# Stores one step behind, and two products ahead of their copies, in the first layer of a streaming-encoder trunk

## The chip, the cores and the metric

The kernel runs on one core of a Trainium2 chip. The metric is the device time of one execution in microseconds. An execution of the kernel before is described by its median over three runs and by one execution that the hardware profiler recorded; the rows below are of that one.

## What is computed

The reference is a trunk of two layers over 2048 frames of 1024 channels, in float32. The change lies in the first layer, a gated mixer, and in the lines that prepare the second:

```
h = rms_norm(x, a_norm_g)
u, v, z = split(h @ w_in, 3)                    # 3 x 2048 channels
u = gelu(u);  v = layer_norm(gelu(v), ln_g, ln_b)
mixed = einsum('hts,bgshc->bgthc', w_m, v)      # 16 heads, groups of 128 frames
y = u * (mixed + b_s) * silu(z)
x = x + y @ w_out
```

`w_m` is a 128x128 matrix per head, zero where a frame would see a later chunk of 64. The second layer is attention over bands of nine chunks, and a final norm follows; it is not changed.

## The kernel before

**Products.** Each float32 operand is split into a high and a low float32r part (`split`, L264: ScalarE copies the high part, VectorE subtracts for the low one), and each product is three matmuls (`mm3`, L105 to L108: high x high, high x low, low x high). The large products of the first layer use seven sub-products in place of eight (a Strassen scheme): `PH = (1, 2, 6, 5, 7, 4, 3)` names the phases, and each phase has its own combination T of weight quarters and its own combination S of input blocks.

**Steps.** The first layer is one list of steps (weight block n, phase, row pair j), written out by hand and run by `run_steps` (L461). One step is one accumulator, or two in the phases 1 and 2 of block 0, which serve the blocks 0 and 1 together: 12 matmuls of 128x512 each (24 in the output product). Three steps ahead (`LOOK`) the S of a step is prepared: transposed and split from the normed x (`s_split`, L409) in block 0, or loaded (`s_load`, L402) later on. Each split S is also stored to HBM (`hsd`, L416), since the blocks 1 to 5 read it again. Blocks 0 and 1 give v, which is stored after the gelu (`done_v`, L435; store at L440). Blocks 2 to 5 give u and z for 512 channels each; they need v mixed over the frames.

**Mixing.** `mix` (L614) makes one bank: an accumulator tile of 128 x 2 x 2 x 128, which holds the products of two heads, three matmuls of 128x256 each. In its loop the three matmuls of a head are followed by the copy of that half to SBUF by ScalarE (L628, scale and bias included), and then come the next head's. There are two such tiles in turn. A bank's result `m` is multiplied into u (`merge_u`, L632, on GpSimd) or into the gate (`done_uz`). `transposes` (L636) turns the finished y and stores it (L643). The output product reads y back and stores the new residual x1 (`done_out`, L842; store at L851).

**Late work.** `later(k, f)` (L425) keeps f for k steps; `flush(s)` (L428) runs what is due at the start of the products of step s. Evictions follow their product at once; gelus are a step late, stores of v two steps late with their statistics.

**Order.** Nearly all loads and stores are issued by SyncE's queue (SP), in program order. The listed order isn't the final one: a scheduler places the instructions of each engine by data and by listing, so that what is listed later may still stand earlier. An instruction that waits for its data holds those behind it on its engine. Buffers are rings: six S tiles (L242), four raw weight tiles, eight T tiles, four transpose tiles, four accumulators for products.

**Preparing the second layer.** `load_scaled` (L169) loads a weight block, multiplies it by a norm gain on GpSimd and stores the scaled block for later use (L178). Five such calls are listed within the output product of the first layer; later calls come from the second layer.

Of the kernel before, what the change touches and what calls it, by code (L numbers as in the profile page):

```python
# [17 lines left out]
P = 128  # L18
# [5 lines left out]
TB = T // P  # L24
# [9 lines left out]
def trunk_kernel(  # L34
# [19 lines left out]
    nc = tc.nc  # L54
# [4 lines left out]
    x1d = [dram.tile([T, D], F32, name=f"x1d{t}") for t in range(NT)]  # L59
# [45 lines left out]
    def mm3(ps, lh, ll, rh, rl, first, last):  # L105
        mm(ps, lh, rh, start=first, stop=False)  # L106
        mm(ps, lh, rl, start=False, stop=False)  # L107
        mm(ps, ll, rh, start=False, stop=last)  # L108
# [19 lines left out]
    def norm_transpose(name, src, wide, pool, tag, bufs):  # L128
# [37 lines left out]
            norm(b)  # L166
        return [(th[:, k, :], tl[:, k, :]) for k in range(KD)], block

    def load_scaled(src, name, gain=None, keep=None):  # L169
        raw = sh.tile([P, 1024], F32, tag="raw", name=f"raw_{name}", bufs=4)  # L170
        nc.sync.dma_start(raw[:], src)
        if gain is not None:
            k = gain.shape[1]
            r3 = raw[:].rearrange("p (k c) -> p k c", k=k)
            nc.gpsimd.tensor_tensor(
                r3, r3, gain.broadcast_to([P, k, 1024 // k]), op=ALU.mult
            )
            nc.sync.dma_start(keep, raw[:])  # L178
        return raw

    def load_split(*args):
# [37 lines left out]
    with ExitStack() as actx:  # L219
# [8 lines left out]
        vd = {  # L228
            (c, r, q): dram.tile([P, 2, 512], F32, name=f"vd{c}_{r}_{q}")
            for c in range(4) for r in range(2) for q in range(4)  # L230
        }
        ytd = {
            (r, c, j): dram.tile([P, 2, 512], F32, name=f"ytd{r}_{c}_{j}")
            for r in range(2) for c in range(2) for j in range(NJ)
        }
# [3 lines left out]
        def acc_tile(name):  # L239
            return ca.tile([P, 512], F32, tag="acc", name=name, bufs=25)  # L240

        def s_tile(name):  # L242
            return ca.tile([P, 2, 4, P], F32R, tag="S", name=name, bufs=6)
# [20 lines left out]
        def split(hi, lo, src, key=None):  # L264
            ins = nc.scalar.copy(hi, src)
            if key:
                in_order(key, ins)
            nc.vector.tensor_tensor(lo, src, hi.bitcast(F32), op=sub)  # L268
# [130 lines left out]
        def s_views(t):  # L399
            return [(t[:, 0, k, :], t[:, 1, k, :]) for k in range(4)]  # L400
# [8 lines left out]
        def s_split(ph, j, rows):  # L409

            pt = ptp[0].tile([P, 4, P], F32, tag="t0", name=f"t0_{ph}_{j}", bufs=4)
            for k in range(4):
                tpose(pt[:, k, :], rows[:, k * P : k * P + P], ident[:])
            t = s_tile(f"S0_{ph}_{j}")
            split(t[:, 0], t[:, 1], pt[:], "S")
            nc.sync.dma_start(  # L416
                hsd[ph, j][:], t[:].rearrange("p a k c -> p a (k c)").bitcast(F32)
            )
            return s_views(t)


        late = []
        now = [0]

        def later(steps, f_):  # L425
            late.append((now[0] + steps, f_))

        def flush(s):  # L428
            now[0] = s
            due = [f_ for at, f_ in late if at <= s]  # L430
            late[:] = [x_ for x_ in late if x_[0] > s]
            for f_ in due:
                f_()

        def done_v(n, r, c, j, t):  # L435
            ch = 2 * n + c

            def close():
                nc.vector.bn_stats(vst[:, r, j, ch, :], t)
                nc.sync.dma_start(vd[ch, r, j // 2][:, j % 2, :], t)  # L440

            later(1, lambda: nc.scalar.activation(t, t, AF.Gelu_apprx_tanh))
            later(2, close)
# [17 lines left out]
        def run_steps(steps, ts, prep, act, events):  # L461


            left = {}
            for s in range(-LOOK, len(steps)):
                for f_ in events.get(s, []):
                    f_()
                if s >= 0:
                    act(s, *steps[s], left.pop(s))
                if s + LOOK < len(steps):  # L470
                    left[s + LOOK] = prep(*steps[s + LOOK])
                for f_ in ts.get(s, []):
                    f_()
# [62 lines left out]
        def block_d(j):  # L536
            s_split(5, j, hb.pop(j)[:, 0:512])
# [76 lines left out]
        def mix(n, r, q, part):  # L614
            vh, vl = mixp[n, r, q]
            ws = wsp[n]
            if part == 0:
                mt[n, r, q] = up[0].tile([P, 2, 512], F32, tag="m", name=f"m{n}_{r}_{q}", bufs=4)
            m = mt[n, r, q]
            px = up[1].tile([P, 2, 2, P], F32, tag="mx", name=f"mx{n}_{r}_{q}_{part}", bufs=2)  # L620
            for i in range(2):
                h = 2 * part + i
                c = slice(h * P, h * P + P)
                mm3(
                    px[:, i], ws[:, 0, h, :], ws[:, 1, h, :], vh[:, :, c], vl[:, :, c], True, True
                )
                hh = (n - 2) * 4 + h
                nc.scalar.activation(  # L628
                    m[:, :, c], px[:, i], AF.Identity, scale=0.5, bias=bsh[:, hh : hh + 1]
                )  # L630
# [5 lines left out]
        def transposes(n, r, j, y):  # L636
            pt = up[1].tile([P, 4, P], F32, tag="ty", name=f"ty{n}_{r}_{j}", bufs=2)
            for h in range(4):
                tpose(pt[:, h, :], y[:, h * P : h * P + P], ident[:])
            yo = up[2].tile([P, 512], F32, tag="yo", name=f"yo{n}_{r}_{j}", bufs=2)  # L640
            nc.scalar.copy(yo[:], pt[:].rearrange("p a b -> p (a b)"))
            fc = n - 2
            nc.sync.dma_start(ytd[r, fc // 2, j][:, fc % 2, :], yo[:])  # L643

        def done_uz(n, r, c, j, t):
            tt = nc.vector.tensor_tensor
            if c == 0:
                later(1, lambda: nc.scalar.activation(t, t, AF.Gelu_apprx_tanh))
                if r == 0:
                    u0[n, j] = t  # L650
                    return
                later(2, lambda: tt(t, t, z1[n][:, j, :], op=mul))
            else:
                th = up[2].tile([P, 512], F32, tag="th", name=f"th{n}_{r}_{j}", bufs=2)
                m = mt[n, 1, j // 2][:, j % 2, :] if r else u0[n, j]
                eng = nc.gpsimd if r else nc.vector
                later(1, lambda: nc.scalar.activation(th[:], t, AF.Tanh, scale=0.5))
                later(2, lambda: nc.vector.scalar_tensor_tensor(t, th[:], 1.0, t, op0=add, op1=mul))
                later(2, lambda: eng.tensor_tensor(t, t, m, op=mul))
                if r == 1:  # L660
                    return
            later(4, lambda: transposes(n, r, j, t))
# [92 lines left out]
        for n in range(2, 6):  # L755
# [3 lines left out]
            for r, offs in ((0, (5, 9, 13, 17)), (1, (22, 25, 28, 31))):  # L759
                for q, o in enumerate(offs):  # L760
# [4 lines left out]
                    if r == 0:  # L765
                        for i in range(2):
                            j = 2 * q + i
# [5 lines left out]
        def act_in(s, n, ph, j, views):  # L773
            flush(s)
            for m in (0, 1) if n == 0 and ph in (1, 2) else (n,):
                ps = pmm.tile([P, 512], F32, tag="mm", name=f"P{m}_{ph}_{j}")
                product(ps, views, tops[m, ph])
                if m < 2:
                    evict(m, ph, j, ps, done_v, None if m else c22_0)
                else:  # L780
                    evict(m, ph, j, ps, done_uz, uz_c22(m))
# [60 lines left out]
        def done_out(n, r, c, j, t):  # L842
            blk = 2 * j + r
            cs = slice(c * 512, c * 512 + 512)
            xr = acc_tile(f"xr{blk}_{c}")
            nc.sync.dma_start(xr[:], x[blk * P : (blk + 1) * P, cs])
            rs = slice(blk % TB * P, (blk % TB + 1) * P)

            def close():
                (tg if r and c else tv)(t, t, xr[:], op=add)  # L850
                nc.sync.dma_start(x1d[blk // TB][rs, cs], t)  # L851

            later(1, close)

# [26 lines left out]
        for c in range(3):  # L881
            at(nin + 26 + 2 * c, lambda c=c: load_scaled(*kqz_source(0, 0, c)))
        for c in range(2):
            at(nin + 32 + 2 * c, lambda c=c: load_scaled(*v_source(0, 0, c)))
# [8 lines left out]
        def prep(n, ph, j):  # L893
            return prep_out(ph, j) if n == "o" else prep_in(n, ph, j)

        def act(s, n, ph, j, views):
            if n == "o":
                act_out(s, ph, j, views)
            else:
                act_in(s, n, ph, j, views)  # L900

        run_steps(steps, ts, prep, act, events)
        flush(1 << 30)
        blocks[0](3)
        px.close()

# [487 lines left out]
```

## Time and profile before

| | us |
|---|---|
| median of three runs | 2729.15 |
| lowest and highest | 2726.96, 2733.49 |
| the profiled execution, whole | 2726.1 |
| its span, first to last instruction | 2724.1 |

The first layer's blocks take about the first half of the span, up to about 1390 us. Around the span lie 2.0 us. A row of the page's groups gives a source line, an engine, the operation with the tiles it writes and reads, and then the busy time; a row of a timeline gives the start and the length in microseconds, the engine, the line and the operation, and in brackets how long the engine had been idle before it and what ended that. PE stands for TensorE's matmuls, PEld for its weight loads, DVE for VectorE, ACT for ScalarE, POOL for GpSimd, SPq for SyncE's queue.

### The profile page before, as it was taken

What the parts mean: (1) busy time and instruction counts of PE and PEld (TensorE: products, weight loads), DVE (VectorE), ACT (ScalarE), POOL (GpSimd) and SP (SyncE); (2) the same over time, 40 slices, a digit from 0 to 9 for tenths busy, and PEclk for the clock granted to TensorE, in tenths of its full rate; (3) what the DMA queues carried; (4) which work ended last, traced back from release to release, by engine and by line L of the source; (5) the groups of instructions that cost most, each with busy time, mean ns of one, the idle gap of its engine ahead of it and who ended that gap; (6) DMA issues with size and microseconds to landing.
All of it is one profiled execution on the core that took longest, in us unless ns stands there. A gap on an engine that the chain in (4) does not pass through costs nothing.

```text
span 2724.1 us, 39971 instructions
## 1 busy us (share of the span) xinstructions
PE 2666.4 (98%) x14176; PEld 2268.7 (83%) x14176; DVE 1932.2 (71%) x3211; ACT 1274.6 (47%) x2244; POOL 711.9 (26%) x767
## 2 busy tenths in 40 slices
PE   8999999999999999999999999999999999999997
PEld 6788878878788888777888888899988999889996
DVE  5655666766667667666767666877778777787777
ACT  5422243433433434232245554566655666556663
POOL 3512123141231422632034430211202112021111
PEclk9999999999999999999999999999999999999999
DMA  8899988886877868758767655544454444453332
GB/s 291 307 335 332 324 324 314 286 299 234 309 263 249 312 232 323 270 200 290 258 220 233 217 181 178 166 146 153 154 174 164 148 151 154 150 160 119 115 112 70
DMA packets 209190, 607.16 MB, mean 223 GB/s; under 512 B 24288, under 2 KB 24288, under 8 KB 208992
## 3 DMA queue, kind: packets, MB, share of 16 engines
q1 hardware_dynamic: 208992, 604.62, 64.5%
q8 instruction: 113, 1.85, 0.3%
q14 instruction: 85, 0.70, 0.1%
HBM read 466.11 MB, written 127.93 MB: 218 GB/s over the span
## 4 chain that ended last, share of the span: by engine, by line
PE 42%; DVE 5%; DMA 4%; POOL 1%; issue 1%; ACT 1%; SPq 0%; DVEq 0%; POOLq 0%; ACTq 0%
PE pj L106 6%; PE pj L107 6%; PE pj L108 6%; PE s L1065 4%; PE tp L1104 4%; PE pv L1131 4%; PE bo L108 2%; PE bo L107 2%; PE bo L106 2%; PE vp L108 2%; PE vp L106 2%; PE vp L107 2%; DMA xr<-in_x 1%; DMA bx_b<-x1d 1%; DMA A<-ytd 1%
## 5 line engine op out<-in xcount | busy, mean ns | idle before, releaser
L106 PE MATMUL P<-T,S 128*128 128x512 f32 x1248 | 497.4, 399 | 6.5 <-ACT x L376 4.5
L108 PE MATMUL P<-T,S 128*128 128x512 f32 x1248 | 490.6, 393 | 0.0
L107 PE MATMUL P<-T,S 128*128 128x512 f32 x1248 | 489.5, 392 | 1.1 <-DVE T L268 1.1
L1084 POOL TENSOR_SCALAR pr<-pr,sl 128x640 f32<-128x640 f32 (+4 forms) x256 | 199.1, 778 | 754.6 <-DVE sl L1083 662.0
L1080 ACT ACTIVATE pr<-pr,nm 128x640 f32<-128x640 f32 (+4 forms) x256 | 195.5, 764 | 270.6 <-DVE nm L1073 269.0
L106 PE MATMUL pj<-hh_b,wh_b 128*128 128x512 f32 x768 | 311.5, 406 | 0.7 <-ACT hh_b L160 0.7
L107 PE MATMUL pj<-hl_b,wh_b 128*128 128x512 f32 x768 | 302.2, 394 | 0.0
L108 PE MATMUL pj<-hh_b,wl_b 128*128 128x512 f32 x768 | 301.3, 392 | 0.0
L108 PEld LDWEIGHTS P<-T,S 128*128 128x128 f32 x1248 | 235.5, 189 | 50.5
L106 PEld LDWEIGHTS P<-T,S 128*128 128x128 f32 x1248 | 236.1, 189 | 49.2 <-ACT x L376 4.7
L107 PEld LDWEIGHTS P<-T,S 128*128 128x128 f32 x1248 | 236.3, 189 | 43.9 <-DVE T L268 1.3
L1108 DVE TENSOR_TENSOR pt<-tp,pt 128x640 fp32r<-128x640 f32 (+4 forms) x256 | 188.8, 737 | 60.0 <-ACT pt L1107 57.4
L1073 DVE CUSTOM_DVE_ANT_0 pr<-s,bias 128x640 f32<-128x640 f32 (+4 forms) x256 | 188.3, 735 | 45.9 <-PE s L1065 42.2
L108 PEld LDWEIGHTS pj<-hh_b,wl_b 128*128 128x128 f32 x768 | 144.2, 188 | 33.2
L1107 ACT CAST pt<-tp 128x640 fp32r<-128x640 f32 (+4 forms) x256 | 159.1, 622 | 22.5 <-PE tp L1104 17.2
L1104 PE MATMUL tp<-ident,pr 128*128 128x128 f32 x1120 | 164.8, 273 | 3.3 <-DVE pt L1108 1.6
L106 PEld LDWEIGHTS pj<-hh_b,wh_b 128*128 128x128 f32 x768 | 144.6, 188 | 19.6 <-ACT hh_b L160 0.9
L1104 PEld LDWEIGHTS tp<-ident,pr 128*128 128x128 f32 x1120 | 134.6, 140 | 31.3 <-issue 3.1
L107 PEld LDWEIGHTS pj<-hl_b,wh_b 128*128 128x128 f32 x768 | 145.0, 189 | 17.4
L106 PE MATMUL vp<-wh_bv,hh_b 128*128 128x256 f32 x512 | 148.0, 289 | 0.8 <-ACT hh_b L160 0.8
L108 PE MATMUL vp<-wh_bv,hl_b 128*128 128x256 f32 x512 | 145.4, 284 | 0.1
L107 PE MATMUL vp<-wl_bv,hh_b 128*128 128x256 f32 x512 | 144.8, 283 | 0.0
(216 smaller groups left out, 6063.3 us busy)
## 6 DMA issues: line engine op xcount, KB each, us to landing
S<-hsd SPq DMA_DIRECT2D x288, 512.0 KB, 4.9
rw<-in_w_a SPq DMA_DIRECT2D x108, 512.0 KB, 5.8
raw_b<-wk SPq DMA_DIRECT2D x75, 512.0 KB, 4.0
A<-ytd SPq DMA_DIRECT2D x72, 512.0 KB, 5.1
hsd<-S SPq DMA_DIRECT2D x56, 512.0 KB, 4.5
rwo<-in_w_out SPq DMA_DIRECT2D x40, 512.0 KB, 5.3
bias<-reld SPq DMA_DIRECT2D x64, 320.0 KB, 3.2
raw_bo<-in_wb_out SPq DMA_DIRECT2D x36, 512.0 KB, 3.9
```

Of the source, the lines that this page charges most:

```text
L106: mm(ps, lh, rh, start=first, stop=False)
L107: mm(ps, lh, rl, start=False, stop=False)
L108: mm(ps, ll, rh, start=False, stop=last)
L1065: mm(ps[:, sg, :w], q[:, qb * P : (qb + 1) * P], kx[:, koff + sg * w : koff + (sg + 1) * w], start=i == 0, stop=i == 1,)
L1073: nc.vector.tensor_tensor_reduce(out=pr[:, c0:].rearrange("p (a b) -> p a b", a=nseg), in0=ps[:, :nseg, :w], in1=bias[:, c0:].rearrange("p ...
L1080: nc.scalar.activation(pr[:, c0:], pr[:, c0:], AF.Exp, scale=-1.0, bias=nm[:], accum_out=sl[:])
L1084: nc.gpsimd.tensor_scalar(pr[:, c0:], pr[:, c0:], sl[:], 1.0, op0=ALU.mult, op1=ALU.mult)
L1104: tpose(tp[:, b, :], pr[:, b * P : (b + 1) * P], ident[:])
L1107: nc.scalar.copy(oh, tp[:, b0:5, :])
L1108: nc.vector.tensor_tensor(pt[:, 1, b0 + qq : 5 + qq, cs], tp[:, b0:5, :], oh.bitcast(F32), op=ALU.subtract)
L1131: mm(po[:, 0, :], keys(i), pt[:, j, i, :], start=(t == 0 and j == 0 and i == blocks[0]), stop=(j == 1 and i == blocks[-1]),)
```

## The change

In the first layer each store that used to be listed right behind the operation whose result it takes is now listed one step later: the S stores, the v stores, the y stores and the x1 stores. The stores of scaled weights are listed two steps later while the first layer's steps run (`put_off` holds a function then, and is emptied at their end). At the end of the steps, what is still kept is run step by step, so that work which keeps further work is run too. In `mix`, the matmuls of both heads of a bank are listed first, and then the two copies.

```
+    put_off = []
+
     def load_scaled(src, name, gain=None, keep=None):
...
-            nc.sync.dma_start(keep, raw[:])
+            if put_off:
+                put_off[0](lambda: nc.sync.dma_start(keep, raw[:]))
+            else:
+                nc.sync.dma_start(keep, raw[:])
...
             split(t[:, 0], t[:, 1], pt[:], "S")
-            nc.sync.dma_start(
+            later(1, lambda: nc.sync.dma_start(
                 hsd[ph, j][:], t[:].rearrange("p a k c -> p a (k c)").bitcast(F32)
-            )
+            ))
...
                 nc.vector.bn_stats(vst[:, r, j, ch, :], t)
-                nc.sync.dma_start(vd[ch, r, j // 2][:, j % 2, :], t)
+                later(1, lambda: nc.sync.dma_start(vd[ch, r, j // 2][:, j % 2, :], t))
...
-            for i in range(2):
-                h = 2 * part + i
-                c = slice(h * P, h * P + P)
+            hs = [2 * part, 2 * part + 1]
+            cs = [slice(h * P, h * P + P) for h in hs]
+            for i, (h, c) in enumerate(zip(hs, cs)):
                 mm3(
                     px[:, i], ws[:, 0, h, :], ws[:, 1, h, :], vh[:, :, c], vl[:, :, c], True, True
                 )
+            for i, (h, c) in enumerate(zip(hs, cs)):
                 hh = (n - 2) * 4 + h
                 nc.scalar.activation(
...
-            nc.sync.dma_start(ytd[r, fc // 2, j][:, fc % 2, :], yo[:])
+            later(1, lambda: nc.sync.dma_start(ytd[r, fc // 2, j][:, fc % 2, :], yo[:]))
...
-                nc.sync.dma_start(x1d[blk // TB][rs, cs], t)
+                later(1, lambda: nc.sync.dma_start(x1d[blk // TB][rs, cs], t))
...
+        put_off.append(lambda f_: later(2, f_))
         run_steps(steps, ts, prep, act, events)
-        flush(1 << 30)
+        while late:
+            flush(now[0] + 1)
+        put_off.clear()
```

## The prediction

> **What bounds the kernel now.** I read the page first, then the windows by stage, then the waits of TensorE, then the timeline at the places where it waits.
>
> ```profile
> span 2724.1 us, 39971 instructions
> PE 2666.4 (98%) x14176; PEld 2268.7 (83%) x14176; DVE 1932.2 (71%) x3211; ACT 1274.6 (47%) x2244; POOL 711.9 (26%) x767
> ...
> 0.00:50.00 50.00, 40.01 (x177) 32.71 (x178) 26.74 (x35) 29.95 (x49) 14.58 (x25) 0.90 0.75 269
> 50.00:100.00 50.00, 46.97 (x235) 38.80 (x235) 26.43 (x34) 21.79 (x37) 36.49 (x29) 1.00 0.80 297
> 150.00:200.00 50.00, 50.00 (x238) 41.42 (x237) 28.80 (x41) 12.59 (x18) 0.00 (x0) 1.00 0.94 344
> 400.00:500.00 100.00, 100.00 (x470) 81.36 (x469) 66.46 (x81) 34.26 (x55) 35.09 (x24) 1.00 0.86 309
> ```
>
> TensorE is the bound: busy 98% of 2724.1 us. No other engine passes 71%, so work on them costs time only where TensorE waits for it. The windows (width, then busy time of PE, PEld, DVE, ACT, POOL, then granted clock, DMA share, GB/s) show where idle time is left: 10.0 us in the first 50, 3.0 in the next, none from 150 to 200, where the DMA engines are busy 94%. "Busy" hides small losses, because a matmul's row lasts longer than the distance to the next one's start. I therefore count starts: undisturbed, a 128x512 product starts 0.23 us after the last (0.11 to 0.12 for 128x256).
>
> The waits (who waited for whom: total us, times, longest) name the places that the change touches:
>
> ```profile
> PEld mx L106 <- ACT m L628: 26.0, 64, 2.7
> PE mx L106 <- ACT m L628: 6.0, 4, 2.2
> PE P L106 <- ACT x L376: 4.5, 1, 4.5
> PE t L413 <- DVE S L268: 4.8, 3, 2.5
> ```
>
> **Part 1: both products of a mixing bank ahead of its copies.** There are 64 banks (4 widths x 2 x 4 x 2), and 64 weight loads wait for the copy at L628: in each bank, the second product (L106) waits until ScalarE has copied the first half out. One ordinary bank, by starts, and the worst one:
>
> ```profile
> 414.19 0.40 PE L108 MATMUL P<-T,S 128*128 128x512 f32 x1
> 414.46 0.39 PE L106 MATMUL mx<-vh,ws 128*128 128x256 f32 x1
> 414.68 0.28 PE L107 MATMUL mx<-vl,ws 128*128 128x256 f32 x1
> 414.80 0.28 PE L108 MATMUL mx<-vh,ws 128*128 128x256 f32 x1
> ...
> 742.49 0.39 PE L106 MATMUL mx<-vh,ws 128*128 128x256 f32 x1 [2.23 <-ACT m L628]
> 743.70 0.63 PE L106 MATMUL P<-T,S 128*128 128x512 f32 x1
> 744.12 0.63 PE L107 MATMUL P<-T,S 128*128 128x512 f32 x1
> 745.83 0.63 PE L108 MATMUL P<-T,S 128*128 128x512 f32 x1
> ```
>
> The second product starts 0.27 us after the last one instead of 0.23, and the product behind it 0.22 instead of 0.12, since its weights could not be loaded ahead: 0.04 + 0.10 = 0.14 us for each of the 60 banks without idle time in PE's row, 8.4 us. The four others idle 6.0 us; to each I add the 0.10 and the 0.17 by which a row outlasts its start distance (0.39 against 0.22): 6.0 + 4 x 0.27 = 7.1. After the longest, six 128x512 products start 0.43 us apart, twice 0.23, and three 128x256 ones follow at 0.21: 6 x 0.2 + 3 x 0.1 = 1.5 us. Sum: 8.4 + 7.1 + 1.5 = **17.0 us**. In the changed order of instructions all 64 banks have the six products in a row, no copy between, so the wait has no place left. What is late next: the copies. The first copy now follows six products, 0.36 us later. Its readers are the merges on POOL (26% busy) and the gate product, steps later; and the bank comes free for the bank after next, which starts at least one step (2.7 us) on, while two copies take 2 x 0.47 us. I cost the delay at nothing; without that cover it is at most 64 x 0.36 = 23 us, and I take 1 us off for a few places. Bounds: 6.0 (the PE row alone) and 26.0 (the PEld row). I take 16, near the counted 17.
>
> [...] Here a pause of 2.23 us brings products 0.43 us apart for some 3.4 us. [...]
>
> **Part 2: stores one step behind.** It moves 56 stores of S (512 KB), 64 of v, 64 of y, 32 of the output and the 5 scaled weights that are listed in this layer; nothing is added or removed. SP issues in program order, so a store that waits for its data holds every load behind it:
>
> ```profile
> 11.66 0.33 SPq L416 DMA_DIRECT2D hsd<-S  x1
> 12.04 3.55 SPq L499 DMA_DIRECT2D ha<-in_x  x6
> 15.71 9.46 SPq L416 DMA_DIRECT2D hsd<-S  x2
> 25.22 0.42 SPq L499 DMA_DIRECT2D hb<-in_x  x1
> 39.04 0.33 SPq L416 DMA_DIRECT2D hsd<-S  x1
> ...
> 29.52 1.06 ACT L505 ACTIVATE jk<-hb 128x1024 bf16<-128x1024 f32 x1 [2.16 <-DMA hb<-in_x]
> 30.58 1.05 ACT L376 COPY x<-P 128x512 f32<-128x512 f32 x2
> ...
> 26.14 0.60 PE L413 MATMUL t<-ident,ha 128*128 128x128 f32 x4
> 31.20 0.80 PE L106 MATMUL P<-T,S 128*128 128x512 f32 x1 [4.45 <-ACT x L376]
> 41.18 0.63 PE L413 MATMUL t<-ident,hb 128*128 128x128 f32 x4 [0.20 <-DVE ra L508]
> ```
>
> The first store holds six x blocks until 11.66; the third holds x block hb0 until 25.22. ScalarE stands before hb0 until 29.52, the evictions of the first two products stand behind it (30.58), and TensorE, which has four accumulators, idles 4.45 us. In the changed order the six blocks, hb0 and hb1 stand ahead of all stores. hb0 is then the 14th transfer: 14 x 524 KB at the 344 GB/s of the full stretch is 21.3 us, plus 0.7 for the first issue and 2 for landing: 24. Square to 25.1, evictions to 26.2: the product that waited until 31.20 can start at 26.6. Next on the way are the norms:
>
> ```profile
> 31.58 1.29 DVE L512 SCALAR_TENSOR_TENSOR hb<-hb,ra,gab 128x1024 f32<-128x1024 f32 x1 [0.73 <-POOL ra L509]
> 36.12 2.30 DVE L512 SCALAR_TENSOR_TENSOR ha<-ha,ra,gab 128x1024 f32<-128x1024 f32 x1 [3.19 <-POOL ra L509]
> 39.75 1.28 DVE L512 SCALAR_TENSOR_TENSOR hb<-hb,ra,gab 128x1024 f32<-128x1024 f32 x1 [0.67 <-POOL ra L509]
> ```
>
> hb0's scaling starts 2.1 us after its square, now at about 26.6 (DVE has ha5 ahead); hb1's ends 9.45 later by these rows, less a split of 0.6 that now stands behind it: 35.5. TensorE gets there at 26.6 + two steps' products (24 x 0.23) and three transposes (1.3) = 33.4 and waits about 2 us where it started at 41.18: a gain of 5.6. Those 2 us may bring a slow stretch of 1.5; I count half: 4.8.
>
> Then three pauses at the transposes and one at a product:
>
> ```profile
> 54.99 0.66 PE L413 MATMUL t<-ident,hb 128*128 128x128 f32 x4 [0.49 <-DVE S L268]
> 88.74 0.66 PE L413 MATMUL t<-ident,hb 128*128 128x128 f32 x4 [1.82 <-DVE S L268]
> 99.20 0.50 PE L106 MATMUL P<-T_hl,S 128*128 128x512 f32 x1 [0.71 <-DVE ra L508]
> 105.58 1.12 PE L413 MATMUL t<-ident,hb 128*128 128x128 f32 x4 [2.45 <-DVE S L268]
> ...
> 76.35 2.53 POOL L292 TENSOR_TENSOR ch<-rw,rw 128x512 f32<-128x512 f32 x2
> 78.83 2.52 POOL L292 TENSOR_TENSOR ch<-rw,ch 128x512 f32<-128x512 f32 x2
> 83.15 1.28 DVE L512 SCALAR_TENSOR_TENSOR hb<-hb,ra,gab 128x1024 f32<-128x1024 f32 x1 [6.78 <-POOL ra L509]
> 96.72 1.23 DVE L268 TENSOR_TENSOR T<-ch,T 128x1024 fp32r<-128x1024 f32 x1 [5.65 <-ACT T L265]
> ```
>
> At 83.15 the norm had stood 6.78 us behind POOL's weight sums (L292). The changed order puts these sums, and their loads, behind the norm. With 0.17 added to each idle time as above I count 0.7 + 2.0 + 0.9 gone, and half of the last with a slow stretch like that after 742 (2.6 + 1.5): 5.6. A wait like that of 96.72, for weights that POOL has still to sum, stays in DVE's queue, and for it I keep the other half. Sum of the start: 4.8 + 5.6 = **10.4 us**; bounds 0 (the new wait at hb1 takes it all) and 14 (all idle rows in this part and their slow stretches). Elsewhere the stores move little: in the changed order on SP none of the y stores changes place against its neighbours and of the output's two do. Of the weight loads 29 come later; the nearest to its product still has its split 64 products, 14.5 us, ahead. Cost: nothing, covered by these 14.5 us.
>
> **Sum.** 16 + 10.4 = 26 us off the profiled execution's 2726.1 us: 2700. The median of the runs shown, 2729.15, lies 3.05 above that execution; from it, **2703 us**.
>
> **Rivals.** (a) The start is given back: from 150 us on the DMA engines are at 94%, and an earlier TensorE meets loads that are no earlier. For it: the row of 150:200. Against it: the first 100 us have 22 us of unused DMA, and three copies of the bias table leave this stretch. Price: the 10.4; 2713. (b) The bank's wait only moves to the next bank's first product, or the orders fall out badly at the output product: 16 is lost, 10 stays: 2719. (c) Slower: the ring of S tiles.
>
> ```profile
> hsd<-S SPq DMA_DIRECT2D x56, 512.0 KB, 4.5
> ```
>
> S tiles come from a ring of six, and in the first 16 steps up to three are taken per step, so six last some two steps of 6.4 us (24 products and ten transposes). A tile is free when its store has landed, and the store is now listed a step later. The stores take 4.5 us from issue to landing; by the chain above each reuse has about 5 us of room. From a landing of 9.5 us on, splits wait, and then the transposes: some 2.5 us at each of the 13 steps that reuse tiles, 33 us against the 26 gained: 2736. Against it: before, these stores land in half of that. (d) The change does nothing: stores find their place by data alone, banks run as before. Against it: the changed order; 2729.
>
> **Chances.** Forecast 0.60 (its own range 2696 to 2709), (a) 0.18, (b) 0.10, (c) 0.07, (d) 0.05. The range that leaves out 2 in 10 takes in (a) and part of (b), and below the bounds of 14 and 17 plus a few us at the output product: 2693 to 2718. This kernel's measurement can tell 0.2%, 5.5 us, from no change. Faster 0.88, same 0.05, slower 0.07.
>
> **What would show it.** Right: no wait of PE or PEld for ACT at L628; TensorE's idle time before 110 us down by some 7 us; the first evictions (L376) near 25; hb loads issued before 10. Wrong: PE waits for S splits in the first 100 us with SP's store landing late; waits for T at phase starts; DMA share over 0.97 from 150 to 400 with PE idle.

## The result and the profile after

The changed kernel takes 2704.01 us in the median of five runs (2699.57 to 2705.59). The kernel before, run beside it, takes 2729.15 (2723.96 to 2734.10). The ratio is 0.9902, with a 95% interval from 0.9887 to 0.9918: 26.7 us less, between 22.4 and 30.8. (Here and below a ratio is turned into microseconds with the median of the kernel before in the same series.) Forecast were 2703 us and 26.

The page of the changed kernel, and its windows over the stretches shown of before (width, busy time of PE, PEld, DVE, ACT, POOL, granted clock, DMA share, GB/s):

```profile
span 2703.7 us, 39985 instructions
PE 2650.0 (98%) x14176; PEld 2267.8 (84%) x14176; DVE 1932.4 (71%) x3211; ACT 1267.2 (47%) x2244; POOL 711.6 (26%) x767
```
```profile
0.00:50.00 50.00, 42.21 (x202) 34.76 (x203) 28.80 (x37) 28.86 (x50) 15.73 (x26) 0.93 0.76 280
50.00:100.00 50.00, 48.73 (x248) 40.83 (x246) 29.75 (x43) 25.47 (x45) 34.78 (x31) 1.00 0.80 295
...
400.00:500.00 100.00, 97.69 (x468) 81.51 (x467) 67.89 (x82) 32.47 (x54) 37.52 (x24) 1.00 0.87 314
```

The share of busy time tells nothing: 98% before and after. The counts do: in the first 50 us TensorE runs 202 matmuls where it ran 177. The stretch from 400 to 500 us, which had no idle time, now has 2.3 us of it. The waits of TensorE for the mixing copy are gone (they were 26.0 us of weight loads, 6.0 of matmuls), and one new wait at a bank stands in their place:

```profile
PE mx L107 <- DVE vl L273: 2.3, 1, 2.3
```

The timeline of TensorE at the bank that waited longest before, and at that new wait:

```profile
727.48 0.28 PE L106 MATMUL mx<-vh,ws 128*128 128x256 f32 x1
...
727.71 0.28 PE L108 MATMUL mx<-vh,ws 128*128 128x256 f32 x1
727.83 0.28 PE L106 MATMUL mx<-vh,ws 128*128 128x256 f32 x1
...
728.07 0.28 PE L108 MATMUL mx<-vh,ws 128*128 128x256 f32 x1
728.19 0.39 PE L106 MATMUL P<-T,S 128*128 128x512 f32 x1
...
439.03 0.39 PE L107 MATMUL mx<-vl,ws 128*128 128x256 f32 x1 [2.31 <-DVE vl L273]
```

Six products start 0.12 us apart and the next large one 0.12 after them: nothing is left of the 2.23 us and of the 0.14 that an ordinary bank lost. The start, on SP's queue, on ScalarE and on TensorE:

```profile
4.06 6.56 SPq L504 DMA_DIRECT2D ha<-in_x  x6
11.56 0.33 SPq L504 DMA_DIRECT2D hb<-in_x  x1
...
16.68 0.33 SPq L504 DMA_DIRECT2D hb<-in_x  x1
18.04 20.14 SPq L421 DMA_DIRECT2D hsd<-S  x6
38.23 0.60 SPq L292 DMA_DIRECT2D rw<-in_w_a  x1
```
```profile
24.76 1.07 ACT L381 COPY x<-P 128x512 f32<-128x512 f32 x2
```
```profile
105.82 1.05 ACT L270 CAST T<-ch 128x1024 fp32r<-128x1024 f32 x1 [5.31 <-POOL ch L297]
106.78 1.05 ACT L510 ACTIVATE jk<-hb 128x1024 bf16<-128x1024 f32 x1
```
```profile
27.36 0.47 PE L106 MATMUL P<-T,S 128*128 128x512 f32 x1
...
36.72 0.63 PE L418 MATMUL t<-ident,hb 128*128 128x128 f32 x4 [2.22 <-DVE hb L517]
...
111.10 0.63 PE L418 MATMUL t<-ident,hb 128*128 128x128 f32 x4 [2.04 <-DVE hb L517]
```

The ha blocks, hb0 and hb1 stand ahead of the first S store, the first evictions start at 24.76 where they started at 30.58, and the product that idled 4.45 us until 31.20 starts at 27.36. Two pauses come at the norms: for hb1 at 36.72, which was forecast, and for hb7 at 111.10, which was not. At hb7 ScalarE stands 5.31 us before its copy of a weight block that POOL has still to sum, and hb7's square comes behind that copy.

To see where time is won and lost, I take the start of the same matmul in two recorded executions and call the difference the **lead** over the recorded execution of before (us, from the rows of the timelines; the last columns are the first and last step of the output product, and the last output rows of the second layer; the kernels are those of the experiments below):

| matmul, its start before | hb1 41.2 | product 110.3 | hb7 119.8 | block 2, 359.9 | 1064.2 | 1386.1 | 2684.4 |
|---|---|---|---|---|---|---|---|
| changed kernel | 4.5 | 10.9 | 8.7 | 8.7 | 23.5 | 18.8 | 20.4 |
| mixing loop alone | 0.1 | 1.5 | 1.5 | 1.5 | 17.4 | 12.9 | 13.9 |
| all stores alone | 4.2 | 10.6 | 8.3 | 8.3 | 7.2 | 4.2 | 2.9 |
| S stores alone | 5.3 | 11.6 | 6.9 | 5.6 | -1.4 | -4.2 | -3.9 |
| all but S stores, with the mixing loop | -0.8 | 0.6 | 0.6 | 0.6 | 17.6 | 12.9 | 15.7 |
| mixing loop and S stores | 4.4 | 11.6 | 5.9 | 4.1 | 17.4 | 12.1 | 15.2 |
| loads ahead, stores in place | 5.1 | 7.1 | 0.3 | -1.6 | -6.7 | -12.3 | -10.4 |
| kernel before, once more | -0.6 | -0.7 | -0.7 | -0.7 | -6.6 | -12.1 | -10.1 |

The last line matters: a second recorded execution of the same program lies 10 us behind the first at the end, so one trace against one trace tells a few microseconds only where the lines of different kernels agree. Up to 360 us the two records of before are 0.7 us apart at the columns shown; the kernel with the mixing loop alone, which runs the code of before up to there, lies 1.5 us off on the other side. So a lead at 360 us is known to a microsecond or two.

### The profile page after: what moved, and what is told of

Its sections match the earlier page's. It is cut to its first block, busy times and chain, and to the rows that moved or that the text cites. A ratio compares the mean times of both kernels' runs of the same rounds, so it can differ in the third digit from the quotient of the medians.

```text
span 2703.7 us, 39985 instructions
## 1 busy us (share of the span) xinstructions
PE 2650.0 (98%) x14176; PEld 2267.8 (84%) x14176; DVE 1932.4 (71%) x3211; ACT 1267.2 (47%) x2244; POOL 711.6 (26%) x767
## 3 DMA queue, kind: packets, MB, share of 16 engines
q8 instruction: 113, 1.85, 0.3%
## 5 line engine op out<-in xcount | busy, mean ns | idle before, releaser
L107 PEld LDWEIGHTS pj<-hl_b,wh_b 128*128 128x128 f32 x768 | 145.5, 189 | 17.4
```

## The experiments

The theory was that of the prediction: two separate gains, one at the banks because the second product waits for the copy that still reads its bank, one at the start because loads stand behind waiting stores on SP. The rivals: that the start is given back later; that the waits only shift; that other stores than those of S carry the gain; that S tiles become short.

**Each part by itself.** Four kernels share one series, in which the kernel before takes 2731.37 us.

```diff
 mixing loop alone: kernel before, and in mix
-            for i in range(2):                # product, copy, product, copy
+            for i, (h, c) in enumerate(zip(hs, cs)):    # both products
+            for i, (h, c) in enumerate(zip(hs, cs)):    # both copies
```


> The kernel before, with only the mixing loop changed: both products of a bank listed ahead of its two copies; every store stays where it was. Theory (the two parts are separate and add up): 14 to 17 us less than the kernel before; TensorE's lead over the kernel before grows only between 365 and 970 us, TensorE's idle time before 120 us stays as it was (some 16 us), and no wait for the copy at the line of the mixing copies is left. Rival 1 (the waits at the banks only shift, and the gain of the whole change came from the start): under 6 us. Rival 2 (only idle rows count, not the late starts): 6 us.

2714.87 us, ratio 0.9933 (0.9920 to 0.9945): 18.3 us less, between 15.0 and 21.9. The lead grows from 1.5 to 17.4 between 360 and 1064 us; the 1.5 before that is spread between executions. Both rivals fall: neither 6 us nor a shift of the waits.

```diff
 all stores alone: the changed kernel with the old mixing loop
-            for i, (h, c) in enumerate(zip(hs, cs)):    # both products, then both copies
+            for i in range(2):                          # product, copy, product, copy
```


> The changed kernel with the mixing loop of the kernel before: all stores a step later, the copies again between the products. Theory: 8 to 11 us less than the kernel before, all of it won before 120 us; the 64 waits of weight loads for the mixing copies are back. Rival (the start is given back where the DMA engines are at 94 per cent): the lead is there at 120 us and gone by 400 us, 0 to 3 us less in all.

2724.20 us, ratio 0.9973 (0.9962 to 0.9984): 7.4 us less, between 4.4 and 10.4. The 64 waits of weight loads are back (27.4 us in all). The lead of 8.3 us at 120 us is still 8.3 at 360. The stretch with DMA engines at 94% takes nothing back; this rival falls. By time the two parts add up within their intervals: 18.3 + 7.4 = 25.7 against 26.7 for both.

```diff
 S stores alone: kernel before, and in s_split
-            nc.sync.dma_start(hsd[ph, j][:], ...)
+            later(1, lambda: nc.sync.dma_start(hsd[ph, j][:], ...))
```


> The kernel before, with only the stores of the split S (512 KB, 56 of them) a step later; the stores of v, y, x1 and of scaled weights stay, and so does the mixing loop. Theory (the S stores at the head of the SP queue held the loads of the x blocks, and they alone make part 2): within 3 us of the kernel with all stores later, 8 to 11 us less than before. Rival (the other stores carry a share): 5 us less or under, while the kernel with all stores later keeps its 8 to 11.

2728.79 us, ratio 0.9991 (0.9979 to 1.0003): 2.5 us less, between 0.8 more and 5.7 less. The theory that S stores alone make part 2 falls. The lead at 110 us is as high as with all stores (11.6), and 4.7 us of it go at hb7. The timeline of TensorE, then of SP, of this kernel:

```profile
112.85 0.88 PE L413 MATMUL t<-ident,hb 128*128 128x128 f32 x3 [4.52 <-DVE hb L512]
```
```profile
81.69 1.16 SPq L440 DMA_DIRECT2D vd<-c  x1
89.23 0.92 SPq L416 DMA_DIRECT2D hsd<-S  x2
90.20 1.89 SPq L440 DMA_DIRECT2D vd<-c  x2
92.14 0.68 SPq L287 DMA_DIRECT2D rw<-in_w_a  x1
```

and SP with all stores later:

```profile
81.34 2.18 SPq L445 DMA_DIRECT2D vd<-c  x2
83.58 0.82 SPq L292 DMA_DIRECT2D rw<-in_w_a  x1
92.62 0.92 SPq L421 DMA_DIRECT2D hsd<-S  x2
```

With the v stores (`vd`) in their old place, the next weight block (`rw`) stands behind three of them and behind two S stores, of which the first waits 6.3 us for its split, and goes at 92.14 in place of 83.58. POOL's weight sums wait for the block, ScalarE's copy of those weights waits for the sums, and the square of hb7 stands behind that copy: hb7's scaling starts at 111.42, with all stores later at 110.04. With 1.3 us more lost just behind, this is the 2.7 us by which the two lines of the table differ at block 2. The chain is read from the rows; it was not tried by itself.

```diff
 all but S stores: the changed kernel, and in s_split
-            later(1, lambda: nc.sync.dma_start(hsd[ph, j][:], ...))
+            nc.sync.dma_start(hsd[ph, j][:], ...)
```


> The changed kernel with the stores of the split S back in their old place; the mixing loop and all other stores as changed. Theory: as the kernel with the mixing loop alone, 14 to 17 us less than before, and TensorE's 4.45 us pause at 31 us is back. Rival (the other stores carry a share of the gain, or cost something at the output product): at least 4 us away from the kernel with the mixing loop alone, in either direction.

2714.73 us, ratio 0.9929 (0.9916 to 0.9942): 19.4 us less, between 15.8 and 22.9, as the mixing loop alone. The pause at 31 us is back. TensorE's row:

```profile
32.01 0.79 PE L106 MATMUL P<-T,S 128*128 128x512 f32 x1 [4.87 <-ACT x L381]
```

So the S stores alone bring 2.5, the others alone 19.4 - 18.3 = 1.1, both together 7.4. The intervals are too wide to tell 2.5 + 1.1 from 7.4. The leads at block 2 say it better: 4.1 to 5.6 in the two kernels in which the S stores move and the v stores do not, 0.6 where all but the S stores move, 8.3 to 8.7 where all do. That each group holds the queue while the other is freed is how I read this.

**What the wait at the bank is, and what holds the start.** The kernel before takes 2733.05 us in this series.

```diff
 two tiles: kernel before, and in mix, with the old order of listing
-            px = up[1].tile([P, 2, 2, P], F32, tag="mx", ..., bufs=2)
+                px = up[1].tile([P, 2, P], F32, tag="mx", ..., bufs=2)   # one per head
```


> The kernel before with its listing (product, copy, product, copy), but each head's product has an accumulator tile of its own, 128 x 2 x 128, in a bank of its own, two in turn. Theory (the second product waited because the copy was still reading the bank that it writes to): the 64 waits go although no copy is listed later, and the time is that of the kernel with the mixing loop alone, 14 to 20 us less than before. Rival (it is the listing: what is listed behind a copy stays behind it): the waits stay, no gain.

2714.26 us, ratio 0.9935 (0.9921 to 0.9950): 17.8 us less, between 13.7 and 21.6. The waits for the copy are gone though each copy is still listed between the products. The bank's timeline:

```profile
388.56 0.28 PE L108 MATMUL mx<-vh,ws 128*128 128x256 f32 x1
388.68 0.28 PE L106 MATMUL mx<-vh,ws 128*128 128x256 f32 x1
...
388.91 0.28 PE L108 MATMUL mx<-vh,ws 128*128 128x256 f32 x1
389.03 0.39 PE L106 MATMUL P<-T,S 128*128 128x512 f32 x1
```

That the two halves share one tile is what costs, not that a copy is listed ahead: in the kernel before 64 weight loads wait for the copy (26.0 us), though product and copy are in disjoint halves; with a tile for each head none does. Why a shared tile makes them wait, this run does not show.

```diff
 loads ahead: kernel before, no store moved; in run_steps and for block_b
+                if s < 0:
+                    for f_ in ts.pop(s, []):      # the x loads, ahead of the first S store
+                        f_()
-            norm_at(e - 1, e, block_b, j)
+            norm_at(-LOOK if j < 2 else e - 1, e, block_b, j)
```


> The kernel before, with no store and no copy moved: instead the loads of the x blocks ha2 to ha7, hb0 and hb1 are listed ahead of the first S store. Theory (part 2 works by the loads that stood behind waiting stores on SP): the pause of 4.45 us at 31 us is gone as in the changed kernel, TensorE's lead at 110 us is 6 us or more. As the v stores stay in their old place and the mixing banks wait longer when TensorE comes earlier (both seen with the S stores alone), 1 to 6 us less than before in all. Rival (the stores' own transfers at the start cost the time, not the order on SP): the pause at 31 us stays, lead at 110 us under 2 us, no gain.

2735.82 us, ratio 1.0011 (1.0001 to 1.0020): 3.0 us more, between 0.3 and 5.5. The lead at 110 us is 7.1, as the theory wants, and the pause at 31 us is gone; the rival falls for the first 40 us. But a gain was expected, and there is none: at hb7 TensorE waits 6.62 us, and the lead is 0.3.

```profile
119.49 0.87 PE L413 MATMUL t<-ident,hb 128*128 128x128 f32 x3 [6.62 <-DVE hb L515]
```
```profile
113.24 1.04 ACT L265 CAST T<-ch 128x1024 fp32r<-128x1024 f32 x1 [8.90 <-POOL ch L292]
...
114.67 1.06 ACT L508 ACTIVATE jk<-hb 128x1024 bf16<-128x1024 f32 x1
```

hb7's load goes at 104.71 here, at 97.83 in the changed kernel. But what ended last ahead of hb7's square is, as in the changed kernel, ScalarE's wait for POOL's weight sums, 8.90 us in place of 5.31: the weight blocks go at 97.25 and 100.94 here, at 93.34 and 97.07 there. Winning the first pause was worth nothing here, where the queue then held the loads that the last x block needs (lead 7.1 at 110 us, 0.3 at hb7).

```diff
 mixing loop and S stores: both edits above in the kernel before
```


> The kernel before with the mixing loop as changed and the S stores a step later; the stores of v, y, x1 and of scaled weights stay. Theory (the S stores alone gave little because the mixing banks took their gain back, by longer waits, and the v stores held loads): with the banks free of waits the lead of some 6 us at 120 us is kept, 22 to 25 us less than before, and 2 to 4 us over the changed kernel, for the v stores. Rival (the S stores are worth 2 to 3 us however the banks wait): 18 to 21 us less, as the mixing loop alone.

2711.08 us, ratio 0.9927 (0.9910 to 0.9943): 20.0 us less, between 15.6 and 24.6. The interval does not part the two. The leads do, at the start: 4.1 at block 2 against 8.7 in the changed kernel, lost at hb7 and just behind (a wait of 5.47 there, against 2.04). The expectation that free banks would keep the lead of the S stores was wrong: it was lost ahead of the banks. At 1064 us the changed kernel leads by 6.1 more, 4.6 of it from here; the rest I have not traced.

```diff
 kernel before, once more: no edit
```


> The kernel before, unchanged, profiled once more, to see how far two recorded executions differ by stage. All profiles of the changed kernels lose 3 to 5 us against the recorded execution of before between 1100 and 1480 us. Theory (that execution was a quick one there, it lies 3 us under its median): this one is 3 to 5 us slower than it, and the difference arises between 1100 and 1480 us. Rival (every change of the first layer costs 3 to 5 us at the output product): the two agree within 1.5 us there.

2735.97 us in this one execution, 9.9 more than the recorded one. It loses 5.5 us between 1064 and 1386, as the changed kernel does (4.7). So the loss of lead there, 2.8 to 5.5 us in every line of the table, may be put down to the first recorded execution, which lost little there. It is not the whole account: in four of the five kernels that are not in the table, the loss over this stretch is none (two tiles; S stores on ScalarE's queue), 7.8 us (S stores two steps later) and 8.2 us (split ahead). The stretch differs from execution to execution, and one trace of a kernel can't show what a change does to it. The second execution also loses 5.9 us at the banks, which the theory had not said. The waits of this execution, against the 26.0 and 6.0 us of the first:

```profile
PEld mx L106 <- ACT m L628: 32.6, 64, 3.2
PE mx L106 <- ACT m L628: 12.0, 8, 2.7
```

What a bank waits differs from execution to execution; the prediction counted in the one of the two that has less of it.

**Further along the same lines.** The kernel before takes 2731.56 us in this series.

```diff
 norms ahead of sums: the changed kernel, and in block_c
-            nc.gpsimd.tensor_tensor(s3[:], a11, b1_, op=sub)
+            behind(nc.gpsimd.tensor_tensor(s3[:], a11, b1_, op=sub), last["pow"])
```


> The changed kernel, with the three block sums on POOL ordered behind the norms' powers that are listed before them. Theory (the pause that was forecast at hb1, 2.2 us at 36.7 us in the changed kernel, comes from POOL's sums ahead of its power): this pause goes, the transposes of hb1 start near 34.5. In the end 0 to 3 us less than the changed kernel, that is 25 to 30 less than before: the pause at 111 us (hb7) can take the gain back. Rival (the pause is set by the landing of hb1): it stays at 36.7 us, no change.

2713.76 us, ratio 0.9924 (0.9903 to 0.9945): 20.8 us less than before, between 15.0 and 26.5, and in the trace 6 us behind the changed kernel. Expected were 25 to 30; by time alone the kernel isn't told from the changed one (22.4 to 30.8). The wait at hb1 is gone, as the theory says (its transposes start at 34.83), so its cause is POOL's order. A larger one follows, at hb2. TensorE, and what ScalarE waited for ahead of hb2's square:

```profile
51.96 0.63 PE L418 MATMUL t<-ident,hb 128*128 128x128 f32 x4 [3.84 <-DVE hb L517]
```
```profile
46.28 1.05 ACT L270 CAST T<-rw 128x1024 fp32r<-128x1024 f32 x1 [10.13 <-DMA rw<-in_w_a]
```

SP issues those weights at 40.96, where the changed kernel does at 38.23, since its six S stores before them take until 40.91. One wait less at TensorE, and the S stores end later and hold the queue longer; why they wait longer I have not traced.

```diff
 S stores two steps later: the changed kernel, and in s_split
-            later(1, lambda: nc.sync.dma_start(hsd[ph, j][:], ...))
+            later(2, lambda: nc.sync.dma_start(hsd[ph, j][:], ...))
```


> The changed kernel with the S stores two steps later in place of one. Theory (the six S tiles have room for one step more, and SP is still held by an S store from 84 to 92 us): within 3 us of the changed kernel, hb7's load some 1 to 2 us earlier. Rival (the ring of S tiles, forecast rival c: the tile is held until its store has landed): splits wait for tiles in the first 130 us, TensorE's pauses there grow by 5 us or more, 5 to 30 us slower than the changed kernel.

2707.54 us, ratio 0.9906 (0.9889 to 0.9923): 25.7 us less, between 21.0 and 30.3, the same as the changed kernel. hb7's load goes at 94.44 in place of 97.83, and the lead at hb7 is 9.9 us. The ring of S tiles does not tie even with a step more: TensorE's one wait for a split before 130 us, 2.0 us ahead of its first product, is there in the changed kernel too (2.1). The forecast's rival (c) falls.

```diff
 S stores on ScalarE's queue: the changed kernel, and in s_split
-            later(1, lambda: nc.sync.dma_start(hsd[ph, j][:], ...))
+            later(1, lambda: nc.scalar.dma_start(hsd[ph, j][:], ...))
```


> The changed kernel with the S stores, a step later as there, issued by ScalarE's queue in place of SP's. Theory (what costs time at the start is loads behind waiting stores on SP): hb7's load is issued 5 us or more earlier than in the changed kernel (97.8 us), the pause at 111 us is gone, 2 to 6 us less than the changed kernel. Rival 1 (the stores hold ScalarE's evictions in the same way): pauses of TensorE for evictions in the first 130 us, slower than the changed kernel by 3 us or more. Rival 2 (loads drawn ahead on a free SP, the bias tables among them, take the DMA engines): TensorE waits for weights or x blocks in the first 400 us.

2729.12 us, ratio 0.9983 (0.9971 to 0.9995): 4.6 us less than before, between 1.4 and 7.9, and so some 22 more than the changed kernel. Rival 2 holds: the lead is -6.2 us at 120 us and -15.3 at block 2, and the DMA engines are busy 99% of the time from 50 to 70 us (93% in the changed kernel). Of rival 1 TensorE shows 0.5 us: ScalarE's evictions do stand behind its stores, once for 5.3 us, but TensorE waited for an eviction only once. With SP freed of the S stores, thirteen copies of the bias table (`reld`) slip in ahead of the third phase's first weights. SP, POOL, TensorE:

```profile
29.36 6.67 SPq L754 DMA_DIRECT2D reld<-in_rel  x5
...
45.49 3.10 SPq L754 DMA_DIRECT2D reld<-in_rel  x4
...
55.22 4.43 SPq L754 DMA_DIRECT2D reld<-in_rel  x4
59.76 0.53 SPq L292 DMA_DIRECT2D rw<-in_w_a  x1
```
```profile
78.33 2.48 POOL L297 TENSOR_TENSOR ch<-rw,rw 128x512 f32<-128x512 f32 x2 [12.06 <-DMA rw<-in_w_a]
```
```profile
86.44 0.87 PE L418 MATMUL t<-ident,hb 128*128 128x128 f32 x3 [8.91 <-DVE hb L517]
```

POOL waits 12.06 us for weights with hb4's norm behind it, and TensorE 8.91 us for the norm. I read this as the bias copies holding up the weights; no run takes the copies alone out of the way. On that reading the waiting stores had also kept loads that nobody needs yet behind those that are needed.

```diff
 split ahead: the changed kernel, and in mix_prep, at the scaling of a v pair
+                if "vl" in last:
+                    behind(ins, last["vl"])       # VectorE's split of the pair before
```


> The changed kernel, with one order more on VectorE: the scaling of the next v pair stands behind the split of the pair before it. All kernels with the changed mixing loop show one pause there, 2.3 to 3.7 us near 439 us (2.3 in the changed kernel): the low part of a v pair stands on VectorE behind the scaling of the next pair, which waits for its load. Theory: that pause goes and no other comes, TensorE keeps its lead there, 2 to 4 us less than the changed kernel, 27 to 31 less than before. Rival (the pair's buffer is free only then, so that the wait moves to the next bank): a pause of 2 us or more at a neighbouring bank, no change within 2 us.

2704.14 us against 2733.04 of the kernel before in its series, ratio 0.9893 (0.9876 to 0.9909): 29.2 us less, between 24.9 and 33.9. The pause at 439 us is gone and no neighbour has one (the expectation put it at 2.3 to 3.7 us in all kernels with the changed loop; in the traces it runs from 0.3 to 3.6, and with the S stores on ScalarE's queue there is none); between block 2 and 1064 us this kernel's lead grows by 17.4 us (7.5 to 24.9), the changed kernel's by 14.8. At the end of its trace it has 18.0, by losses at the output product. The ratio is the best of all, but its interval covers that of the changed kernel: not shown to beat it.

## The prediction, point by point

**Part 1, 16 us.** Right in mechanism, and the size lies within the interval: 18.3 us (15.0 to 21.9) by itself, 17.8 with a tile for each head. How close it came is in part luck: the second execution of before loses 5.9 us more at the banks than the one in which the 17.0 were counted. In the trace of the changed kernel the banks' stretch gives 14.8 us, and 17.4 where the wait at 439 us is mended; 17.0 were counted. The microsecond taken off "for a few places" stood for a late copy. It was another thing: the low part of a v pair stood on VectorE behind a pair whose load had not landed.

**Part 2, 10.4 us.** Right in mechanism, high in size: 7.4 us (4.4 to 10.4) by time, 8.7 us of lead at 120 us. To hb1 4.8 were forecast and 4.5 came, with errors that offset each other. The product at 31.20 was forecast at 26.6 and came at 27.36, and hb1 was forecast ready at 35.5 and was ready at 36.57, so that the new wait has nearly the forecast length (2.22 us against 2) but comes about 1 us late. The 2 us for landing in the forecast of hb0 are a term that no run shows: from issue to landing the hb loads take 5.5 us in the median before and 6.2 in the changed kernel, and hb0's square, forecast at 24, starts at 23.71 there. Of the 0.75 us that half a slow stretch was to cost, nothing came. POOL's order as the cause of this wait is shown. For the later pauses 5.6 were forecast: the lead grew by 6.4 to 110 us, and the wait for hb7, which the prediction did not see, took 2.2 back. Its cause, weights that POOL has still to sum, is the one for which the prediction kept half of the pause at 105.58; that pause went whole, and the wait came one x block later.

**What the prediction left out.** It counts the stores of v among those that move, but no term weighs them: the rows of SP at the start that it reads are S stores and loads, and "Elsewhere the stores move little" looks at the stores of y and of the output. The S stores by themselves bring 2.5 us (-0.8 to 5.7), against 7.4 (4.4 to 10.4) for all.

**The rivals.** (a) falls: 8.3 us at 120 us, 8.3 at 360, with the stores alone. (b) falls: no bank waits for a copy any more. A loss at the output product is not shown: the second record of before loses as much there, and the traces differ by some 8 us in that stretch. (c) falls: two steps later are no slower. (d) falls with the result.

**From the record to the median.** The sum was made against an execution 3.05 us under its median, and the difference carried over. The second record shows what such a difference is made of: waits at the banks and at the output product, not a constant. The lead of 20.4 us at the end of the two records, against 26.7 by time, is in the main of this kind: the recorded execution of before lies 3.05 us below its median, that of the changed kernel 1.5 above.

**The marks.** No wait at the mixing copy: seen. First evictions near 25: 24.76. The hb loads before 10: wrong, they went at 11.56 and 16.68, since the six ha loads take SP until 10.62. Idle time before 110 us down by some 7: nearly, 6.4 us came off up to the same product (15.5 to 9.1: 2.2 and 1.8 us in the first two windows, 2.45 at the pause of 105.58), and 2.0 came back at 111. Most of the rest of the lead of 10.9 is the granted clock: half for 13.7 us of this stretch before, for 6.8 us after, which, with products 0.43 us apart in place of 0.23, is worth about half the difference, 3.4 us.

## What to carry to other kernels

Here a product into one half of an accumulator tile waited for the copy out of the other half (64 weight loads, 26.0 us); list all products of a tile ahead of its copies (18.3 us here), or give each a tile (17.8 us), and count the late weight loads and starts as well as the idle rows (17 us here, 6 of them idle). In a queue that issues in order (here SP, which two S stores held for 9.46 us from 15.71 on, with hb0 behind them), look at all the stores that can wait, not only at those of the largest group: the S stores alone gave 2.5 us, the others alone 1.1, both 7.4 (the leads at the end of the start bear this out, the intervals of the times don't part it). And a queue freed of waiting stores isn't best by itself: here, with the S stores on ScalarE's queue, it let in thirteen loads that were not yet needed, and the kernel was some 22 us slower than the changed one. Before a trace is compared with another stage by stage, record the kernel before twice.

## What the hardware did that was not expected

A pause of about two microseconds brings a stretch of products 0.43 us apart in some places and not in others. It did after 2.23 us in the kernel before, and after 2.13 us at the bank near 443 us with mixing loop and S stores; it did not after 2.31 us at 439 us in the changed kernel. The first large products after the pause start 0.23 to 0.27 us apart, and the slow ones begin 1.67 us after its end (mixing loop and S stores):

```profile
443.40 0.39 PE L107 MATMUL mx<-vl,ws 128*128 128x256 f32 x1 [2.13 <-DVE vl L268]
...
445.07 0.63 PE L107 MATMUL P<-T,S 128*128 128x512 f32 x1
```

In the slow stretches the recorded granted clock is at half. In the records of before and of the changed kernel its changes lie whole multiples of 3.41 us apart (the first and the last of before, at 6.31 and 2716.49 us, 794 of them). These are the windows of that width around the three pauses, two each (kernel before, mixing loop and S stores, changed kernel):

```profile
740.17:743.58 3.41, 1.18 (x7) 1.00 (x7) 2.00 (x3) 2.27 (x4) 0.00 (x0) 1.00 1.03 410
743.58:747.00 3.42, 3.42 (x11) 2.75 (x11) 3.42 (x5) 0.99 (x2) 2.42 (x2) 0.50 0.40 159
```
```profile
441.55:444.96 3.41, 1.56 (x9) 1.43 (x10) 3.00 (x5) 1.64 (x3) 0.00 (x0) 1.00 0.97 371
444.96:448.38 3.42, 3.42 (x9) 2.69 (x9) 0.00 (x0) 0.24 (x1) 0.00 (x0) 0.50 0.80 302
```
```profile
434.50:437.91 3.41, 2.21 (x11) 1.59 (x9) 3.41 (x6) 0.59 (x1) 0.00 (x0) 1.00 1.02 416
437.91:441.33 3.42, 2.30 (x12) 2.02 (x13) 2.26 (x3) 1.29 (x3) 0.00 (x0) 1.00 0.97 367
```

The first pause lies whole in one window (TensorE busy 1.18 of 3.41 us), the second has 1.85 us in one, and each time the next window runs at half clock. The third is cut by an edge into 1.20 and 1.11 us, and no window at half clock follows. In the records of before and of the changed kernel, between 20 and 2690 us, TensorE idles 1.93 us or more in 11 windows at full clock, and each of them is followed by one at half clock; in the other 1538 it idles 1.86 us or less, and none is. The window with 1.85 us above is followed by half clock, and one with 1.86 us in the changed kernel, at 1229.81, is not: the rows show no sharp limit. What goes with the fall in them is the idle time in one window, not the length of the pause. As an estimate from these rows, a pause of about two microseconds is worth its length and, where most of it falls into one window, another 1.7 us (half of 3.41); from the lengths of the pauses alone the two cases can't be told apart.
